# A streaming-encoder layer on one core: one source order for four engines through all 22 matrix blocks, block sums on VectorE, value loads issued by ScalarE

## The chip, the cores and the metric

The kernel runs on one core of one Trainium2 chip. The metric is the device time of one execution in microseconds (us). Before the change the median of 3 runs is 2679.69 us (2674.99 to 2684.86). The engines are called as the profile calls them: PE is TensorE (matmuls; PEld is its weight load), DVE is VectorE, ACT is ScalarE, POOL is GpSimd, SP is SyncE, which here only issues transfers.

## What is computed

One layer on 2048 tokens of width 1024, all float32:

```python
hn = rmsnorm(h, norm_mix_g[l])
proj = hn @ w_in[l]
...
h = h + jnp.concatenate([y_pool, y_dn], axis=-1) @ w_out[l]
m = rmsnorm(mem, mem_norm_g[l])
h = h + memory_cross_attention(rmsnorm(h, norm_xattn_g[l]), m, w_xq[l], w_xk[l], w_xv[l], w_xo[l])
h = h + sqrelu_mlp(rmsnorm(h, norm_mlp_g[l]), w_up[l], w_down[l])
return rmsnorm(h, final_norm_g)
```

`y_pool` is a multi-scale trailing mean, `y_dn` a gated delta rule in chunks. The cross-attention has 256 memory tokens and 4 heads. The MLP is `relu(h @ w_up) ** 2 @ w_down` with an inner width of 4096.

## The kernel before, in words

**First part (to about 873 us).** Projection, convolution, delta rule and the small memory products. The change does not touch it.

**Second part: 22 blocks.** What is left is 22 products of 1024 x 1024 x 1024, here called blocks 0 to 21 (`macros`, lines 872 and 873). Blocks 0 and 1 are the output projection (`o`) of token halves 0 and 1, blocks 2 and 3 the attention scores (`s`), blocks 4 and 5 the product with values and output weights (`v`). Then come, for each token half, four pairs of an up block (`u`) and a down block (`d`): blocks 6 to 13 for half 0, blocks 14 to 21 for half 1.

**Seven steps a block.** Each block is computed by Strassen's scheme in Winograd's form: seven products of 512 x 512 x 512 instead of eight, in the order 1, 2, 6, 7, 5, 4, 3 (`ORDER`). I call the steps of a block index 0 to 6, as the code does. Each float32 operand is split into a high and a low part that PE takes at full rate, and each product is three matmuls: a step is 4 column tiles `t` = 0 to 3 of 12 matmuls, 48 in all. For a step the other engines must do this:

- `loads(n)` (line 883): SP fetches the operand tiles `x` and `t`, two steps ahead. The pool of `t` has 3 buffers.
- `prep(n)` (line 919): ACT casts the two operands to their high parts `sh` and `th` (4 casts of 128 x 1024), DVE subtracts for the low parts `sl` (line 939) and `tl` (line 941). They go to one of two buffer sets (`win`), so a step's operands can be written only when PE has finished the step before the previous one. For the second token half of `s` and `v` the low part `tl` is not computed again: the first half stored it (`lo_s`, `lo_v`), and POOL issues its load (line 933).
- `chains(n)` (line 985): the matmuls into two groups of four PSUM tiles, A and B, and after each `t` an `evac_...` function that adds the result to where it belongs, mostly on DVE (lines 1027, 1044, 1047, 1065).

**Sums.** Steps of index 2 to 5 need sums of quarters of both operands. `adds(k, part)` (line 946) makes those of the left operand, in four parts of two 128 x 1024 operations: on DVE up to block 6 (`NA` is 6) and for `d` blocks, on POOL for the later `u` blocks. `sums(key, ...)` (line 136) makes those of the right operand in 8 units: POOL issues two loads into a tile `cb`, four 128 x 256 operations follow, on DVE up to block 6 and on POOL later, and POOL issues the store to `sums_...`. The keys are `s`, `v`, `n0`, `n1` (normed activations) and `w0` to `w3` (slices of `w_down`). The dictionary `plan` (lines 1149 to 1159) says at which block and index each unit stands.

**Transposes.** In blocks 1 to 6 PE also transposes the previous block's result (`turned`, line 1119); ACT and DVE copy the transposes out (`nr...`), into the same PSUM pools that B uses.

**Who sets the order.** Up to block 6 the order of PE, ACT, DVE and POOL is the order of the source (`step_fixed`, line 1185): within `t` = 0 and 1 of step n the parts of `prep(n + 1)`, then the copies of the transposes, the evacuation of the previous `t`, and so on. From block 7 on (`step_free`, line 1243) only PE keeps the source's order; a scheduler orders the other engines when the kernel is built. In both cases the order is fixed before the run, and each engine takes its instructions one after the other.

```python
    with tc.manual_schedule(engines={E_.PE}):
        with tc.manual_schedule(engines={E_.Activation, E_.DVE, E_.Pool}):
            for n in range(1, 7 * (NA + 1)):
                step_fixed(n)
            close_fixed()
        for n in range(7 * (NA + 1), len(steps)):
            step_free(n)
```

The last `d` block of each half (blocks 13 and 21) also norms the rows and stores them (lines 1048 to 1054): a square on ACT, a power on POOL (line 103), two multiplications on DVE (line 1053) a row tile.

Of the kernel before, what the change touches and what calls it, by code (L numbers as in the profile page):

```python
# [8 lines left out]
F32 = mybir.dt.float32  # L9
# [23 lines left out]
def hymba_layer(ctx: ExitStack, tc: tile.TileContext, x, mem, norm_mix_g, w_in, w_pool, pool_scale, conv_w,  # L33
# [885 lines left out]
    def prep(n):  # L919
# [10 lines left out]
        for i in range(2):  # L930
            T.append([wtile(w_, a, f"{a}_{nm}_{i}", F32R) for a in ("th", "tl")])
            if known:
                nc.gpsimd.dma_start(T[i][1].bitcast(F32), lo_d[kind][LO[j], i])
# [12 lines left out]
    def adds(k, part):  # L946
# [3 lines left out]
        eng = nc.vector if kind == "d" or k <= NA else nc.gpsimd  # L950
# [87 lines left out]
    def evac_add(n, j, t, ps):  # L1038
# [9 lines left out]
        if kind == "d" and g == DFF // D - 1 and j in (4, 3):  # L1048
            jk = jp.tile([P, D], BF16, tag="jk", name=f"fj{sb}_{r + t}")
            rs = rms_scale(jk, h_, f"f{sb}_{r + t}")  # L1050
            for i, gf in enumerate(mac[kind, sb, g]["gf"]):
                hv = h_[:, i * TB:(i + 1) * TB]
                nc.vector.scalar_tensor_tensor(hv, hv, rs, gf, ALU.mult, ALU.mult)
            nc.sync.dma_start(out[sb * D + (r + t) * P:sb * D + (r + t + 1) * P, :], h_)
# [95 lines left out]
    dense = (4, 4, 4, 5, 5, 5, 6, 6)  # L1150
    late = (3, 3, 4, 4, 5, 5, 6, 6)
    full = (2, 2, 3, 3, 4, 4, 5, 5)
    for k, where in (("s", [(0, i) for i in (1, 2, 2, 3, 3, 4, 4, 5)]),
                     ("v", [(b, i) for b in (1, 3) for i in (3, 4, 5, 6)]),
                     ("w0", [(2, i) for i in (1, 3, 4, 5)] + [(6, i) for i in (3, 4, 5, 6)]),
                     ("n0", [(5, i) for i in dense]), ("w1", [(7, i) for i in full]),
                     ("n1", [(8, i) for i in late]), ("w2", [(9, i) for i in full]), ("w3", [(11, i) for i in full])):
        for at in where:
            plan.setdefault(at, []).append(k)
# [7 lines left out]
    def sum_units(i, idx, t=None):  # L1167
# [4 lines left out]
        for k in todo:  # L1172
            if k not in gens:
                gens[k] = sums(k, side_tile, nc.vector if i <= NA else nc.gpsimd, {"s": 3, "n0": 2}.get(k, 1),
                               4 if k in ("v", "w0") else 0)
            next(gens[k])
# [8 lines left out]
    def step_fixed(n):  # L1185
        k, idx = divmod(n, 7)
        mc = macros[k]
        loads(n + 2)
        if idx == 5:
            open_rows(k + 1)  # L1190
        pr = prep(n + 1)
# [4 lines left out]
        for t, ev in enumerate(chains(n)):  # L1196
            if t < 2:
                next(pr, None)
# [9 lines left out]
            if t == 1:  # L1208
# [21 lines left out]
            if idx == 6 and k < NA and t > 1:  # L1230
                adds(k + 1, t - 2)
# [10 lines left out]

    def step_free(n):
        k, idx = divmod(n, 7)
        if n + 2 < len(steps):
            loads(n + 2)
        if n + 1 < len(steps):
            for _ in prep(n + 1):
                pass
        if idx == 0:  # L1250
            if k > NA + 1:
                open_rows(k)
            adds(k, 0)
            adds(k, 1)
        elif idx == 1:
            adds(k, 2)
            adds(k, 3)
        sum_units(k, idx)
        for ev in chains(n):
            after(after(after([ev])))  # L1260
# [54 lines left out]
```

## Time and profile before

| what | value |
|---|---|
| median of 3 runs | 2679.69 us |
| the profiled execution's own time | 2678.6 us |
| its span in the trace | 2676.9 us |
| PE busy | 2558.5 us (96%) |
| DVE busy | 1949.6 us (73%) |
| ACT busy | 1383.3 us (52%) |
| POOL busy | 812.7 us (30%) |
| mean granted clock of PE | 0.98 |

How to read it: PE is busy nearly all the time, so what can be lost or won at its present work is the rest. The profiled execution took 1.7 us more than its span, and 1.1 us less than the median. Busy shares are means over both parts; what a stage waits for is read block by block.

### The profile page before, as it was taken

The page shows a single profiled execution, that of the slowest core. Times are in us where ns is not written, and L with a number is a line of the kernel's source. Part 1 is how long each engine was busy: PE and PEld are TensorE (multiplying, and loading weights), DVE is VectorE, ACT ScalarE, POOL GpSimd, SP SyncE. Part 2 cuts the span into 40 slices and gives each one's busy share as a digit, 9 for nine tenths or more (in the row PEclk, how much of TensorE's full clock was granted, in tenths as well). Part 3 has the DMA queues.
Part 4 walks back from the last instruction along what each step waited for, and adds up shares of the span by engine and source line. Part 5 has one row for each costly group of instructions (what it writes and reads, how often), then busy time and mean ns, then how long its engine had stood idle before and what let it go on. Part 6 is the DMA issues. An engine that isn't in the chain of part 4 may idle for free.

```text
span 2676.9 us, 35124 instructions
## 1 busy us (share of the span) xinstructions
PE 2558.5 (96%) x12822; PEld 2153.5 (80%) x12822; DVE 1949.6 (73%) x2537; ACT 1383.3 (52%) x2286; POOL 812.7 (30%) x863
## 2 busy tenths in 40 slices
PE   7999999999999899998989899999998999999998
PEld 6887789789778788887868788887887888888887
DVE  6865775675685888878657777878688685868666
ACT  7435534635634455875536546363554636455453
POOL 4432455541421311110021477884202101020100
PEclk9999999999999999999989999999999999999999
DMA  4335246234225999988998658673335434233322
GB/s 145 89 105 187 79 146 214 75 107 150 83 84 184 338 342 364 328 319 323 326 351 281 217 182 274 205 249 129 126 128 193 167 108 160 95 127 123 99 99 103
DMA packets 250743, 495.58 MB, mean 185 GB/s; under 512 B 35445, under 2 KB 105674, under 8 KB 250570
## 3 DMA queue, kind: packets, MB, share of 16 engines
q1 hardware_dynamic: 188538, 382.17, 41.9%
q0 software_dynamic: 26048, 90.19, 9.7%
q10 hardware_dynamic: 35984, 20.98, 2.8%
q8 instruction: 100, 1.64, 0.3%
q14 instruction: 73, 0.60, 0.1%
HBM read 371.64 MB, written 121.63 MB: 184 GB/s over the span
## 4 chain that ended last, share of the span: by engine, by line
PE 59%; DVE 8%; DMA 6%; ACT 4%; issue 4%; POOL 2%; POOLq 0%; DVEq 0%; SPq 0%; ACTq 0%
PE A L1009 28%; PE B L1009 21%; DMA t<-vwo_d 1%; DVE tl L941 1%; PE pcm L98 1%; PE pcm L99 1%; PE pcm L97 1%; DVE sl L939 1%; DMA sums_w<-cb_w 1%; DVE cac L385 1%; PE px L498 1%; DMA sums_n<-cb_n 1%; ACT sh L936 1%; DMA cb_n<-n_d 1%; DVE xb L466 1%
## 5 line engine op out<-in xcount | busy, mean ns | idle before, releaser
L1009 PE MATMUL A<-th,sh 128*128 128x512 f32 x1392 | 547.7, 393 | 11.7 <-DVE vr L1044 11.4
L1009 PE MATMUL A<-tl,sh 128*128 128x512 f32 x1392 | 544.0, 391 | 1.4 <-DVE tl L941 0.8
L1009 PE MATMUL A<-th,sl 128*128 128x512 f32 x1392 | 543.6, 391 | 0.0
L1009 PE MATMUL B<-tl,sh 128*128 128x512 f32 x1056 | 416.3, 394 | 21.5 <-DMA tl<-lo_v 10.5
L1009 PE MATMUL B<-th,sh 128*128 128x512 f32 x1056 | 415.7, 394 | 12.6 <-ACT nrs L1137 6.6
L1009 PE MATMUL B<-th,sl 128*128 128x512 f32 x1056 | 415.3, 393 | 0.0
L941 DVE TENSOR_TENSOR tl<-t,th 128x1024 fp32r<-128x1024 f32 x278 | 391.1, 1407 | 12.1 <-ACT th L937 12.1
L937 ACT CAST th<-t 128x1024 fp32r<-128x1024 f32 x306 | 320.6, 1048 | 49.2 <-DMA t<-sums_w 19.1
L1009 PEld LDWEIGHTS A<-th,sh 128*128 128x128 f32 x1392 | 262.6, 189 | 66.1 <-issue 12.1
L1009 PEld LDWEIGHTS A<-tl,sh 128*128 128x128 f32 x1392 | 262.8, 189 | 55.9 <-DVE tl L941 1.6
L939 DVE TENSOR_TENSOR sl<-x,sh 128x1024 fp32r<-128x1024 f32 x166 | 218.5, 1316 | 121.4 <-ACT sh L936 121.4
L1009 PEld LDWEIGHTS A<-th,sl 128*128 128x128 f32 x1392 | 262.4, 188 | 54.8
L936 ACT CAST sh<-x 128x1024 fp32r<-128x1024 f32 x166 | 173.9, 1048 | 214.3 <-PE B L1009 116.0
L1009 PEld LDWEIGHTS B<-tl,sh 128*128 128x128 f32 x1056 | 200.9, 190 | 66.0 <-DMA tl<-lo_v 10.9
L1009 PEld LDWEIGHTS B<-th,sh 128*128 128x128 f32 x1056 | 201.1, 190 | 56.0 <-ACT nrs L1137 6.8
L1009 PEld LDWEIGHTS B<-th,sl 128*128 128x128 f32 x1056 | 201.0, 190 | 42.0
L936 ACT CAST sh<-c 128x1024 fp32r<-128x1024 f32 x96 | 100.8, 1050 | 226.6 <-PE A L1009 121.2
L97 PE MATMUL pcm<-hhi_x,wh_in 128*128 128x512 f32 x512 | 208.1, 406 | 0.2 <-ACT wh_in L90 0.2
L99 PE MATMUL pcm<-hhi_x,wl_in 128*128 128x512 f32 x512 | 205.0, 402 | 2.3 <-DVE wl_in L91 2.2
L98 PE MATMUL pcm<-hlo_x,wh_in 128*128 128x512 f32 x512 | 204.1, 399 | 0.0
L939 DVE TENSOR_TENSOR sl<-c,sh 128x1024 fp32r<-128x1024 f32 x96 | 126.1, 1313 | 68.1 <-ACT sh L936 68.0
L385 DVE SCALAR_TENSOR_TENSOR cac<-raw,vec,cac 128x512 f32<-128x512 f32 x144 | 129.3, 898 | 2.3
(361 smaller groups left out, 4651.9 us busy)
## 6 DMA issues: line engine op xcount, KB each, us to landing
ws_in<-in_w_in_dram SPq DMA_DIRECT2D x72, 512.0 KB, 3.8
x<-in_w_up_dram SPq DMA_DIRECT2D x64, 512.0 KB, 4.4
t<-sums_n SPq DMA_DIRECT2D x64, 512.0 KB, 4.7
t<-sums_w SPq DMA_DIRECT2D x64, 512.0 KB, 3.2
t<-n_d SPq DMA_DIRECT2D x48, 512.0 KB, 4.5
t<-in_w_down_dram SPq DMA_DIRECT2D x48, 512.0 KB, 4.7
cb_w<-in_w_down_dram POOLq DMA_DIRECT2D x64, 256.0 KB, 5.8
sums_w<-cb_w POOLq DMA_DIRECT2D x32, 512.0 KB, 4.2
```

The costliest lines, as they stand in the source:

```text
L97: nc.tensor.matmul(ps, lhsT=lh, rhs=rh, start=first, stop=False)
L98: nc.tensor.matmul(ps, lhsT=lh, rhs=rl, start=False, stop=False)
L99: nc.tensor.matmul(ps, lhsT=ll, rhs=rh, start=False, stop=last)
L385: nc.vector.scalar_tensor_tensor(a5, raw[:, j:j + 512], g_cv[:, j, ch:ch + 1], a5, ALU.mult, ALU.add)
L466: nc.vector.tensor_tensor(xb[:, 0:i, i:32], xb[:, 0:i, i:32], tv, ALU.subtract)
L498: nc.tensor.matmul(px[:, h * P:(h + 1) * P], lhsT=vT[:, h, :], rhs=cur[:, h, :], start=True, stop=True)
L936: nc.scalar.copy(S[i][0], raw[i])
L937: nc.scalar.copy(T[i][0], m["T"][j][i])
L939: nc.vector.tensor_tensor(S[i][1], raw[i], S[i][0].bitcast(F32), ALU.subtract)
L941: nc.vector.tensor_tensor(T[i][1], m["T"][j][i], T[i][0].bitcast(F32), ALU.subtract)
L1009: nc.tensor.matmul(ps, lhsT=l_[:, a0:a0 + P], rhs=r_[:, b0:b0 + TB], start=start and c == 0 and i_ == 0, stop=last and c == 3 and i_ == 2, ...
```

## The change

One body, `step_fixed`, now serves all 22 blocks, and `step_free` is gone. All `adds` go to DVE. Those of `v` and `d` blocks parts 0 and 1 move from the last index of the previous block to index 0 of their own; those of `u` blocks stand in the last index of the block before. At index 1 the copies of the transposes come ahead of the casts. The loads of `lo_v` are issued by ACT. The plan of the sums changes for `v` (second half of its units), `w1`, `w2`, `w3` and `n1`; POOL still computes those from block 7 on. The final norm is cut into two later pieces.

```diff
             if known:
-                nc.gpsimd.dma_start(T[i][1].bitcast(F32), lo_d[kind][LO[j], i])
+                (nc.scalar if kind == "v" else nc.gpsimd).dma_start(T[i][1].bitcast(F32), lo_d[kind][LO[j], i])
...
-        eng = nc.vector if kind == "d" or k <= NA else nc.gpsimd
+        eng = nc.vector
...
-            jk = jp.tile([P, D], BF16, tag="jk", name=f"fj{sb}_{r + t}")
-            rs = rms_scale(jk, h_, f"f{sb}_{r + t}")
...
+            def rest():
+                jk = jp.tile([P, D], BF16, tag="jk", name=f"fj{sb}_{r + t}")
+                rs = rms_scale(jk, h_, f"f{sb}_{r + t}")
+
+                def scaled():
+                    for i, gf in enumerate(mac[kind, sb, g]["gf"]):
...
-                     ("v", [(b, i) for b in (1, 3) for i in (3, 4, 5, 6)]),
...
+    for k, where in (("s", at(0, 1, 2, 2, 3, 3, 4, 4, 5)), ("v", at(1, 3, 4, 5, 6) + at(3, 0, 2, 3, 3)),
+                     ("w0", at(2, 1, 3, 4, 5) + at(6, 3, 4, 5, 6)), ("n0", at(5, 4, 4, 4, 5, 5, 5, 6, 6)),
+                     ("w1", at(7, *range(6)) + at(8, 3, 4)), ("w2", at(8, 5) + at(9, *range(6)) + at(10, 3)),
+                     ("w3", at(10, 4, 5) + at(11, *range(6))), ("n1", at(12, 3, 4, 5) + at(13, *range(5)))):
...
         for t, ev in enumerate(chains(n)):
+            if idx == 1 and t == 0:
+                after(outs)
+                outs[:] = []
...
+            if mc[0] in "dv" and idx == 0 and t > 1:
+                adds(k, t - 2)
...
-            if idx == 6 and k < NA and t > 1:
+            if idx == 6 and more and macros[k + 1][0] not in "dv" and t > 1:
                 adds(k + 1, t - 2)
...
-    with tc.manual_schedule(engines={E_.PE}):
-        with tc.manual_schedule(engines={E_.Activation, E_.DVE, E_.Pool}):
-            for n in range(1, 7 * (NA + 1)):
-                step_fixed(n)
-            close_fixed()
-        for n in range(7 * (NA + 1), len(steps)):
-            step_free(n)
+    with tc.manual_schedule(engines={E_.PE, E_.Activation, E_.DVE, E_.Pool}):
+        for n in range(1, len(steps)):
+            step_fixed(n)
+        close_fixed()
```

**Place 1: POOL in block 5, index 4 to 6, before.** `cb_n` and `sums_n` are units of `n0`, `tl<-lo_v` are the stored low parts that index 6 of the block needs.

```order
L146 DMA cb_n_4_13434<-n_d_90 128x2x256 x2
L171 DMA sums_n_97<-cb_n_2_13392 128x4x256
L933 DMA tl_0_13467<-lo_v 128x1024
L933 DMA tl_1_13470<-lo_v 128x1024
L146 DMA cb_n_5_13496<-n_d_90 128x2x256 x2
L171 DMA sums_n_97<-cb_n_3_13413 128x4x256
```

In the changed kernel the same two loads stand on ACT, right ahead of the casts of the same step (`sh`, `th`):

```order
L933 DMA tl_0_13465<-lo_v 128x1024
L933 DMA tl_1_13468<-lo_v 128x1024
L936 CAST sh_0_13470<-x_36_0_12796 128x1024
L937 CAST th_0_13464<-t_0_13334 128x1024
L936 CAST sh_1_13488<-x_36_1_12798 128x1024
```

The two loads no longer stand behind the store of a unit of `n0`, which waits for DVE.

**Place 2: POOL at the end of block 6, before.** `sums_w_99<-cb_w_7` is the store of the last unit of `w0`, which block 7 needs; `sums_w_100` belongs to `w1`, which block 9 needs.

```order
L171 DMA sums_w_100<-cb_w_0_14560 128x4x256
L146 DMA cb_w_1_14563<-in_w_down_dram 128x2x256 x2
L167 TENSOR_TENSOR cb_w_1_14563<-cb_w_1_14563 128x256
...
L171 DMA sums_w_100<-cb_w_1_14563 128x4x256
L171 DMA sums_w_99<-cb_w_7_14286 128x4x256
L146 DMA cb_w_2_14571<-in_w_down_dram 128x2x256 x2
```

And in the changed kernel:

```order
L171 DMA sums_w_99<-cb_w_6_14199 128x4x256
L171 DMA sums_w_99<-cb_w_7_14284 128x4x256
L146 DMA cb_w_0_14456<-in_w_down_dram 128x2x256 x2
L146 DMA cb_w_1_14459<-in_w_down_dram 128x2x256 x2
L167 TENSOR_TENSOR cb_w_0_14456<-cb_w_0_14456 128x256
```

The store of the last unit of `w0` now stands ahead of all work for `w1`.

**Place 3: DVE at the end of block 13, in the changed kernel.** `x_98`, `x_99` and `n` are quarter sums of block 14, a `u` block, which POOL made before; `L1056` is the final norm (line 1053 before), `L1044` the evacuation of block 13.

```order
L1056 SCALAR_TENSOR_TENSOR vr_7_11933<-vr_7_11933,rs_f_7_18445,gf_1_17866 128x512
L953 TENSOR_TENSOR x_98_0_18290<-x_98_0_18286,x_98_0_18290 128x1024
L953 TENSOR_TENSOR x_98_1_18292<-x_98_1_18288,x_98_1_18292 128x1024
L1044 SCALAR_TENSOR_TENSOR vr_2_11928<-B_2_18211,rv_0_12972,vr_2_11928 128x512
L1056 SCALAR_TENSOR_TENSOR vr_0_11926<-vr_0_11926,rs_f_0_18469,gf_0_17865 128x512
L1056 SCALAR_TENSOR_TENSOR vr_0_11926<-vr_0_11926,rs_f_0_18469,gf_1_17866 128x512
L957 TENSOR_TENSOR n_0_18499<-x_99_0_18385,x_98_0_18290 128x1024
L957 TENSOR_TENSOR n_1_18500<-x_99_1_18387,x_98_1_18292 128x1024
```

Here the sums of the next block stand between the pieces of the norm on one engine; before, they stood on POOL, between its powers.

## Rows read from the trace of the kernel before

**Rows 1.** Stretches by block: us, PE, PEld, DVE, ACT, POOL busy, PEclk, DMA, GB/s.

```profile
962.51:1045.81 83.30, 83.30 (x401) 69.69 (x400) 71.02 (x91) 43.61 (x59) 12.08 (x14) 1.00 0.91 331
...
1130.22:1217.72 87.50, 84.85 (x402) 69.46 (x401) 64.19 (x113) 65.40 (x136) 13.95 (x22) 1.00 0.91 335
1217.72:1309.15 91.43, 84.87 (x402) 70.68 (x401) 70.61 (x94) 43.40 (x64) 2.39 (x4) 0.96 0.92 325
1309.15:1407.90 98.75, 86.59 (x401) 71.62 (x400) 60.16 (x86) 41.91 (x53) 21.94 (x33) 0.93 0.93 333
1407.90:1495.61 87.71, 85.18 (x401) 70.86 (x400) 64.40 (x82) 57.16 (x73) 19.00 (x21) 0.98 0.81 286
...
1495.61:1581.57 85.96, 79.06 (x338) 64.40 (x337) 69.51 (x68) 29.75 (x31) 57.73 (x56) 0.96 0.55 182
...
1657.73:1733.89 76.16, 76.16 (x338) 63.06 (x337) 66.05 (x65) 30.67 (x32) 60.40 (x58) 1.00 0.63 207
...
1810.04:1894.78 84.74, 79.16 (x338) 64.98 (x337) 71.53 (x64) 29.56 (x31) 30.93 (x23) 0.96 0.37 120
...
2047.10:2133.83 86.73, 79.85 (x338) 64.70 (x337) 60.19 (x53) 51.32 (x67) 20.55 (x10) 0.94 0.60 206
```

**Rows 2.** The same view, blocks 19 and 21, down blocks beside which POOL does little.

```profile
2438.45:2514.61 76.16, 76.16 (x338) 63.08 (x336) 62.16 (x65) 30.08 (x32) 5.67 (x2) 1.00 0.29 97
...
2590.81:2667.10 76.29, 76.28 (x337) 62.86 (x335) 61.55 (x70) 31.69 (x43) 3.81 (x6) 1.00 0.27 95
```

**Rows 3.** Waits of PE from 1040 us on: us in total, times, longest.

```profile
PE A L1009 <- DVE vr L1044: 11.4, 2, 5.8
PE B L1009 <- DMA tl<-lo_v: 10.5, 1, 10.5
PE B L1009 <- DVE tl L941: 6.8, 2, 4.2
PE B L1009 <- ACT nrs L1137: 6.6, 1, 6.6
```

**Rows 4.** Chain that ended last, end of block 3: start, us, what.

```profile
1195.39 18.34 DMA t<-vwo_d
```

**Rows 5.** Instructions of POOL in block 5: start, us, what, idle before.

```profile
1361.96 0.53 POOL L933 DMA_DIRECT2D tl<-lo_v  x1 [0.83 <-PE A L1009]
...
1383.07 1.08 POOL L933 DMA_DIRECT2D tl<-lo_v  x2
...
1403.16 1.42 POOL L146 DMA_DIRECT2D cb_n<-n_d  x2 [8.58 <-DMA sums_n<-cb_n]
```

**Rows 6.** Instructions of DVE in block 5.

```profile
1397.39 0.43 DVE L167 TENSOR_TENSOR cb_n<-cb_n 128x256 f32<-128x256 f32 x1 [6.67 <-DMA cb_n<-n_d]
```

**Rows 7.** Instructions of DVE around the start of block 7.

```profile
1499.22 0.41 DVE L170 TENSOR_TENSOR cb_w<-cb_w 128x256 f32<-128x256 f32 x1
```

**Rows 8.** Instructions of POOL around the start of block 7.

```profile
1508.00 0.74 POOL L170 TENSOR_TENSOR cb_w<-cb_w 128x256 f32<-128x256 f32 x1
1509.03 1.53 POOL L171 DMA_DIRECT2D sums_w<-cb_w  x2 [0.30 <-POOL cb_w L170]
```

**Rows 9.** Instructions of DVE in block 11.

```profile
1832.35 3.61 DVE L960 TENSOR_TENSOR c<-n,c 128x1024 f32<-128x1024 f32 x1
```

**Rows 10.** Instructions of POOL in block 11.

```profile
1832.43 2.43 POOL L957 TENSOR_TENSOR n<-x,x 128x1024 f32<-128x1024 f32 x1
```

**Rows 11.** Instructions of DVE between blocks 13 and 14.

```profile
2042.31 3.55 DVE L1053 SCALAR_TENSOR_TENSOR vr<-vr,rs_f,gf 128x512 f32<-128x512 f32 x2
```

**Rows 12.** Groups of instructions of DVE in block 19: busy us, mean ns, idle before.

```profile
L941 DVE TENSOR_TENSOR tl<-t,th 128x1024 fp32r<-128x1024 f32 x14 | 18.9, 1351 | 0.0
...
L1044 DVE SCALAR_TENSOR_TENSOR dr<-A,rv,dr 128x512 f32<-128x512 f32 x16 | 11.8, 748 | 4.4 <-PE A L1009 4.4
...
L953 DVE TENSOR_TENSOR c<-c,c 128x1024 f32<-128x1024 f32 x2 | 2.4, 1224 | 1.3 <-ACT c L1032 1.3
```

**Rows 13.** Stores of yT_d: ns min, median, max of the issue, first and last start.

```profile
L601 ACTq DMA_DIRECT2D yT_d<-yst x16: 366/367/399, 199.9 to 887.5; - x16
```

More of the change, by code (lines that the diff above doesn't have):

```diff
@@ L1048, in evac_add @@
         if kind == "d" and g == DFF // D - 1 and j in (4, 3):
-            jk = jp.tile([P, D], BF16, tag="jk", name=f"fj{sb}_{r + t}")
-            rs = rms_scale(jk, h_, f"f{sb}_{r + t}")
[L1051 to L1054, printed above, removed]
+            def rest():
[3 more added lines that the diff above has]
+                    for i, gf in enumerate(mac[kind, sb, g]["gf"]):
+                        hv = h_[:, i * TB:(i + 1) * TB]
+                        nc.vector.scalar_tensor_tensor(hv, hv, rs, gf, ALU.mult, ALU.mult)
+                    nc.sync.dma_start(out[sb * D + (r + t) * P:sb * D + (r + t + 1) * P, :], h_)
+                return scaled
+            return rest
     def evac_sc(n, j, t, ps):
@@ L1149, in hymba_layer, with at @@
     plan = {}
[L1150 to L1153, printed above, removed]
-                     ("v", [(b, i) for b in (1, 3) for i in (3, 4, 5, 6)]),
[L1155 to L1159, printed above, removed]
+    def at(b, *idx):
+        return [(b, i) for i in idx]
+    for k, where in (("s", at(0, 1, 2, 2, 3, 3, 4, 4, 5)), ("v", at(1, 3, 4, 5, 6) + at(3, 0, 2, 3, 3)),
+                     ("w0", at(2, 1, 3, 4, 5) + at(6, 3, 4, 5, 6)), ("n0", at(5, 4, 4, 4, 5, 5, 5, 6, 6)),
+                     ("w1", at(7, *range(6)) + at(8, 3, 4)), ("w2", at(8, 5) + at(9, *range(6)) + at(10, 3)),
+                     ("w3", at(10, 4, 5) + at(11, *range(6))), ("n1", at(12, 3, 4, 5) + at(13, *range(5)))):
+        for w_ in where:
+            plan.setdefault(w_, []).append(k)
     gens, now = {}, [0]
@@ L1174, in sum_units @@
                 gens[k] = sums(k, side_tile, nc.vector if i <= NA else nc.gpsimd, {"s": 3, "n0": 2}.get(k, 1),
-                               4 if k in ("v", "w0") else 0)
+                               {"v": 4, "w0": 4, "w1": 6, "w2": 7}.get(k, 0))
             next(gens[k])
@@ L1187, in step_fixed @@
         mc = macros[k]
-        loads(n + 2)
+        more = k + 1 < len(macros)
+        if n + 2 < len(steps):
+            loads(n + 2)
         if idx == 5:
             open_rows(k + 1)
-        pr = prep(n + 1)
+        pr = prep(n + 1) if n + 1 < len(steps) else iter(())
         side = 0 < k <= NA
@@ L1241, in close_fixed @@
         after(outs)
[L1243 to L1260, printed above, removed]
     loads(0)
```

## The prediction

> **What bounds the kernel now.** Read the second part block by block. The first view is the table of stretches, one row a block [rows 1]. Block 1 takes 83.30 us with PE busy throughout: that is what a block with transposes costs when nothing makes PE wait. Block 9 takes 76.16 us, the same for a block without them; ten more of blocks 7 to 21 have that length. So PE bounds the blocks at 83.3 and 76.16 us, and a gain can come only from what single blocks take above that: block 3 4.2 us, block 4 8.1, block 5 15.45, block 6 4.4, block 7 9.8, block 11 8.6, block 14 10.6 [rows 1]; together 61.2 us. Block 2 is 1.1 over, block 0 is filled by a start that the change leaves alone. Not all of an excess is idle time: block 5 idles 98.75 - 86.59 = 12.2 us, and the other 3.3 us are matmuls that run longer, at a granted clock of 0.93; in blocks 7, 11 and 14 the clock is 0.96, 0.96 and 0.94. PE stood before these stretches, and a wait that goes takes the slow stretch behind it along.
>
> The second view, the waits of PE, names who ended the idle time: the loads of `lo_v` once for 10.5 us, the evacuations `vr` on DVE twice for 11.4, `tl` on DVE twice for 6.8, the copies `nrs` on ACT once for 6.6 [rows 3]. Then I followed each of these back through the instructions of the engine named. After the last matmul 9.8 us remain (2667.1 to 2676.9) [rows 2].
>
> **Blocks 3 and 4 (12.3 us over).** In block 3 the operand load `t<-vwo_d`, issued at 1195.39, takes 18.34 us [rows 4]; DVE then does late what stands behind it: the sums of block 4, a unit of `v`, the evacuations, and last the operands and copies that PE waits for. The change takes both loads off this place: units of `v` leave index 4 to 6 of block 3 for index 0 to 3, and the two sums (four operations of 1.22 us [rows 12], 4.9 us) go to index 0 of block 4. Three units that stood there move 0.5 MB in and 0.5 MB out each, 3 MB or 9 us at 335 GB/s [rows 1]; two of them fall before the load's landing, so it should land some 6 us sooner, and DVE has 6 us less to do behind it. At index 1 the copies of the transposes now come ahead of the casts. What remains late is DVE in index 0 of block 4, where the sums now stand. I take 10 of 12.3 us; bounds 3 and 12.
>
> **Blocks 5 and 6 (19.9 us over).** In index 3 the loads of `lo_v` are issued when PE frees the buffer, the second at 1361.96; those for index 6 come only at 1383.07, behind a store of `n0` [rows 5], about 10 us after the buffer was free. ACT will issue them on time. The price is issue time on ACT, 0.37 us a load [rows 13], two a step, plus ACT's wait for the buffer, which the casts behind it need anyway; ACT is busy 41.9 of 98.75 us [rows 1], so this is hidden. So the 10.5 us go. But DVE is late next: it stands before a unit of `n0` until 1397.39 [rows 6], and the operands of block 6 come behind that, about 1402. PE will want them at about 1395. The last load of `n0` is issued at 1403.16 after 8.58 us for a store [rows 5], and the first sums of block 6 use a buffer of the same pool. DMA runs at 333 GB/s here, more than in block 4 [rows 1]. So half of it comes back as a wait for the units: I take 9 us; bounds 0 (the units set the pace as before) and 17.
>
> **Block 7 (9.8 us).** DVE finishes the last unit of `w0` at 1499.6 [rows 7], but POOL issues the store only at 1509 to 1510.6, behind two units of `w1` [rows 8]; block 7 needs it. In the new order it stands ahead of them: 10 us earlier. I take 9; bounds 5 and 9.8.
>
> **Block 11 (8.6 us).** DVE's sum of 128 x 1024 takes 3.61 us [rows 9] instead of 1.22 [rows 12], while POOL does one of 2.43 us from 1832.43 on [rows 10]. Those POOL operations (8 in each `u` block from block 8 on) disappear, and are 8 operations of 1.22 us on DVE. A `u` block leaves DVE room: 3 of its 7 evacuations are DVE's, against 7 in a `d` block. I take 8.5; bounds 4 and 8.6.
>
> **Block 14 (10.6 us).** Two multiplications of the final norm take 3.55 us [rows 11] where two of such form take 1.5 [rows 12], again beside POOL's sums. The change removes that, but puts the sums between the pieces of the norm on DVE: index 6 of block 13 gets four evacuations (3.0 us), four subtractions (2 x 1.35 + 2 x 1.22 = 5.1), eight multiplications (6.0) and four sums (4.9), 19 us in a step of 10.88 (a seventh of 76.16). It ends 8 us late. Operands are normally done some 6 us before PE needs them, so about 2 us remain. I take 8.5; bounds 3 and 10.6.
>
> **After the last matmul.** The last evacuations stood behind older norms; take 1 us, bounds 0 and 2.
>
> **What is added.** In index 6 of each down block the sums of the next up block make 3.0 + 5.1 + 4.9 = 13 us of DVE's work in 10.88 us, and index 0 of each down block the same: 2 us late, inside the 6 us. Over a whole block: block 19 keeps DVE busy 62.2 us [rows 2], with four sums more 67.1. In blocks 7, 9, 11 and 13 POOL makes 5 or 6 units beside it. Block 9 of before, with 8 units (60.4 us of POOL), has DVE at 66.05 us, 3.9 more than block 19 [rows 1, 2]; six units are 2.9 us, so 70 of 76.16. I take 1 us for small new waits; bounds 0 and 10.
>
> The Trainium skill (SBUF — State Buffer, "SBUF: two separate sides") speaks against this: it calls the port that VectorE and GpSimd share an exclusive lock, and says that the one that starts second blocks fully. The 3.61 us in block 11 agree. If DVE were always the one that blocks, six units of four operations of 0.74 us alone [rows 8] would cost DVE 17.8 us a block, and 67.1 + 17.8 = 84.9 would pass 76.16. By block 9 POOL mostly loses: its units took 60 us there. I go by the row; the other is the second rival.
>
> **The sum.** 10 + 9 + 9 + 8.5 + 8.5 + 1 - 1 = 45 us. The profiled execution took 2678.6, so 2633.6; the median stands 1.1 above it: 2634.7 us.
>
> **The rivals.**
> - *The transfers bound blocks 3 to 6.* For: 325 to 335 GB/s in three blocks on end [rows 1], loads that take 18 us [rows 4]. Against: block 1 ran at PE's pace with 331 GB/s. Then 10 + 9 come to nothing, and the time is 2653.7.
> - *The lock goes against DVE in the down blocks with units.* Blocks 7, 9 and 11 go 8.7 us over, block 13 with 5 units 5.8: 32 us, 2667. Against: block 9 [rows 1].
> - *No wait is left but block 0's.* All 61.2 + 1.1 us and the tail's 1 go: 2616.
> - *Slower: DVE breaks step.* The place is index 6 of the seven down blocks before an up block (7 to 19), where 13 us stand in 10.88. It decides if DVE comes there already 4 us late, for then operands pass the 6 us of slack. If each costs what the late blocks 7, 11 and 14 cost now, 9.7 us on the mean, that is 68 us: 2703. Against: blocks 9 and 19 show DVE idle 10 us and more [rows 1, 2].
>
> That the order would not change is no rival: the three places above show that it does.
>
> **How the numbers follow.** Forecast 0.65, transfers 0.10, lock 0.10, no wait left 0.10, slower 0.05. A measurement of this kernel can tell about 0.5% (13 us) from no change. The forecast, the first and the third rival are faster by more; the second (0.5%) counts half as faster, half as no change; the last is slower. So 0.90 faster, 0.05 same, 0.05 slower. The terms' lower bounds taken for two of them at once (blocks 5 and 6 none, block 14 3 us) give 2649, and new waits of 10 us 2658; the upper ones 2617. The range 2616 to 2660 takes in these, the forecast, the first and third rival.
>
> **What would show it right or wrong.** Right: blocks 7, 8, 10, 11 and 12 at 76.2 us, no 128 x 1024 operations on POOL after block 6, loads of `lo_v` issued every 11 to 14 us through block 5, block 4 under 86 us, blocks 5 and 6 together 10 to 12 us above 166.6 with DVE waiting for `cb_n`, block 14 about 78. Wrong: a down block over 78 us with `tl` or `vr` as releaser (lock, or broken step), blocks 5 and 6 unchanged (transfers), or a DVE busy time in blocks 7, 9, 11 above 72 us.

## The result, and the profile after

The changed kernel takes 2645.69 us (median of 4 runs, 2643.81 to 2648.08), the kernel before, run beside it on the same chip, 2678.26 us. The ratio is 0.9876 with a 95% interval of 0.9854 to 0.9898: 1.2% faster, well beyond the 0.5% that can be told from no change. The prediction was 2634.7 us with a range of 2616 to 2660: right in its sign and inside its range, 11.0 us too low. Profiled execution against profiled execution (2647.18 to 2633.6) it is 13.6 us: the prediction put the median 1.1 us above the profiled one, and it lies 1.5 below. The profiled execution took 2647.18 us, its span is 2645.4 us, and the mean granted clock 0.988.

The stretches of blocks 3, 4, 5, 6, 7, 11 and 14 after the change, in the columns of [rows 1] (us, busy time of PE, PEld, DVE, ACT and POOL, granted clock, DMA share, GB/s):

```profile
1128.79:1218.70 89.91, 86.19 (x401) 70.33 (x400) 67.20 (x122) 66.59 (x141) 14.71 (x23) 0.98 0.97 352
1218.70:1303.92 85.22, 83.86 (x402) 69.64 (x400) 65.29 (x83) 41.30 (x59) 0.00 (x0) 1.00 0.89 317
1303.92:1393.38 89.46, 86.42 (x401) 71.79 (x400) 53.05 (x77) 40.37 (x50) 13.87 (x19) 0.96 0.91 324
1393.38:1493.61 100.23, 88.55 (x401) 72.47 (x400) 72.74 (x95) 59.77 (x76) 11.76 (x17) 0.93 0.82 287
1493.61:1569.77 76.16, 76.16 (x337) 63.06 (x336) 66.88 (x67) 29.32 (x31) 46.09 (x43) 1.00 0.57 187
...
1798.25:1874.41 76.16, 76.16 (x337) 63.06 (x336) 67.87 (x68) 29.33 (x31) 38.18 (x33) 1.00 0.51 166
...
2026.73:2103.63 76.90, 76.50 (x337) 63.00 (x336) 54.82 (x57) 51.88 (x65) 6.01 (x3) 1.00 0.70 237
```

Read against [rows 1]: blocks 7 and 11 are at the 76.16 us that a block without transposes costs, block 14 0.74 us above; each was 8.6 to 10.6 us over. Block 5 is 9.3 us shorter, but block 6 is 12.5 us longer, and block 3 2.5 us. Taken from first matmul to first matmul, blocks 1 to 6 are 533.1 us before and 533.2 after; blocks 7 to 21 are 1171.5 before and 1143.3 after. So the whole gain, but for 3.4 us in block 0, the start and the tail, lies behind block 6.

Waits of PE from 1040 us on, after the change (us in total, times, longest), against [rows 3]:

```profile
PE ptv L1136 <- DVE vr L1047: 4.5, 1, 4.5
PE A L1009 <- DVE tl L941: 3.7, 1, 3.7
PE A L1009 <- DMA tl<-lo_s: 3.6, 3, 2.7
PE B L1009 <- ACT nrv L1146: 3.5, 1, 3.5
PE B L1009 <- DVE nrv L1150: 3.0, 1, 3.0
```

The wait of 10.5 us for `lo_v` is gone. Three of the waits in its place (`tl`, `vr`, and `nrv` on ACT, 11.7 us) stand in index 0 of block 6, which takes 27.67 us, where PE alone needs 12.57. The rest of block 6's excess is matmuls that run longer after PE stood: PE is busy 88.55 us in it where 83.30 do, at a granted clock of 0.93. Followed back on DVE (start, us, what, idle before and who ended it):

```profile
1392.15 0.42 DVE L167 TENSOR_TENSOR cb_n<-cb_n 128x256 f32<-128x256 f32 x1 [1.17 <-DMA cb_n<-n_d]
...
1405.44 1.22 DVE L957 TENSOR_TENSOR n<-x,x 128x1024 f32<-128x1024 f32 x1
1412.03 1.22 DVE L957 TENSOR_TENSOR n<-x,x 128x1024 f32<-128x1024 f32 x1 [5.37 <-DMA sums_n<-cb_n]
...
1414.89 0.68 DVE L1047 TENSOR_TENSOR vr<-B,vr 128x512 f32<-128x512 f32 x1
```

DVE stands twice behind the units of `n0`: for their fetches, and, 5.37 us long, in the second sum of block 6 (L957), whose result goes to a buffer that a unit still holds until its store has landed. The evacuation `vr`, for which the transposes wait, is queued behind it. POOL shows the pace of the units:

```profile
1380.05 1.42 POOL L146 DMA_DIRECT2D cb_n<-n_d  x2 [5.58 <-DMA sums_n<-cb_n]
...
1391.20 1.42 POOL L146 DMA_DIRECT2D cb_n<-n_d  x2 [4.58 <-DMA sums_n<-cb_n]
...
1401.78 1.42 POOL L146 DMA_DIRECT2D cb_n<-n_d  x2 [8.38 <-DMA sums_n<-cb_n]
```

Each fetch waits for an earlier store to land and free its buffer. The DMA engines are full while this goes on; in stretches of 10 us (columns as above):

```profile
1390.00:1400.00 10.00, 6.31 (x23) 4.52 (x21) 8.14 (x12) 6.45 (x11) 2.19 (x3) 0.88 1.03 402
...
1410.00:1420.00 10.00, 3.12 (x14) 2.18 (x12) 7.86 (x10) 6.21 (x12) 0.75 (x1) 0.73 0.47 177
```

From 1410 us on they are half idle, and PE still stands. That leaves two readings of blocks 5 and 6: the order of work on DVE and the units' chain (called A, C and G below, as they were sharpened), or the transfers (B).

### The profile page after: what moved, and what is told of

The parts are those of the page before. It is cut to its first block, busy times and chain, and to the rows that moved or that the text cites. A ratio compares the mean times of both kernels' runs of the same rounds, so it can differ in the third digit from the quotient of the medians.

```text
span 2645.4 us, 34978 instructions
## 1 busy us (share of the span) xinstructions
PE 2549.4 (96%) x12822; PEld 2148.9 (81%) x12822; DVE 1938.8 (73%) x2593; ACT 1386.1 (52%) x2286; POOL 672.9 (25%) x793
## 4 chain that ended last, share of the span: by engine, by line
PE 66%; DVE 6%; DMA 4%; issue 2%; ACT 2%; POOL 1%; ACTq 0%; DVEq 0%; SPq 0%; POOLq 0%
PE A L1009 33%; PE B L1009 24%; PE pcm L98 1%; PE pcm L99 1%; PE pcm L97 1%; DMA sums_n<-cb_n 1%; DVE cac L385 1%; PE px L498 1%; DMA tl<-lo_s 1%; DVE tl L941 1%; DVE xb L466 1%; DVE sl L939 0%; PE pto L1136 0%; DMA t<-sums_v 0%; PE ptv L1136 0%
## 5 line engine op out<-in xcount | busy, mean ns | idle before, releaser
L941 DVE TENSOR_TENSOR tl<-t,th 128x1024 fp32r<-128x1024 f32 x278 | 355.6, 1280 | 4.0 <-ACT th L937 4.0
L939 DVE TENSOR_TENSOR sl<-x,sh 128x1024 fp32r<-128x1024 f32 x166 | 206.1, 1242 | 75.1 <-ACT sh L936 75.0
L103 POOL TENSOR_TENSOR rs_f<-rs_f,mhalf 128x1 f32<-128x1 f32 x16 | 17.0, 1063 | 628.8 <-ACT rs_f L102 628.8
L939 DVE TENSOR_TENSOR sl<-c,sh 128x1024 fp32r<-128x1024 f32 x96 | 118.8, 1237 | 39.3 <-ACT sh L936 39.3
```

The costliest lines, as they stand in the source:

```text
L103: nc.gpsimd.tensor_tensor(dst, dst, mhalf[:, :dst.shape[-1]], ALU.pow)
L939: nc.vector.tensor_tensor(S[i][1], raw[i], S[i][0].bitcast(F32), ALU.subtract)
L941: nc.vector.tensor_tensor(T[i][1], m["T"][j][i], T[i][0].bitcast(F32), ALU.subtract)
```

## The experiments

Block lengths (first matmul to first matmul, in us, profiled execution) of all kernels; each ratio is against runs of the kernel before on the same chip.

| kernel | median us | ratio (95%) | block 3 | 4 | 5 | 6 | 7 to 21 |
|---|---|---|---|---|---|---|---|
| before | 2678.26 | 1 | 87.45 | 91.45 | 98.81 | 87.69 | 1171.5 |
| changed | 2645.69 | 0.9876 (0.9854 to 0.9898) | 89.92 | 85.21 | 89.47 | 100.23 | 1143.3 |
| e1 first blocks only | 2676.28 | 0.9985 (0.9970 to 1.0000) | 90.69 | 85.23 | 87.09 | 101.36 | 1172.8 |
| e2 MLP only | 2649.18 | 0.9882 (0.9862 to 0.9902) | 87.51 | 92.51 | 96.85 | 90.57 | 1143.3 |
| e3 `n0` units on POOL | 2651.22 | 0.9890 (0.9869 to 0.9912) | 91.05 | 85.22 | 87.27 | 102.06 | 1143.3 |
| e4 no `lo_v` transfers | 2637.42 | 0.9837 (0.9820 to 0.9855) | 90.93 | 86.08 | 83.31 | 94.61 | 1143.3 |
| e5 adds of block 6 later | 2644.87 | 0.9871 (0.9856 to 0.9885) | 90.33 | 85.25 | 89.61 | 96.08 | 1143.3 |
| e6 e4 and e5 | 2637.90 | 0.9843 (0.9827 to 0.9860) | 90.51 | 85.25 | 83.31 | 94.29 | 1143.3 |
| e7 sums of `u` on POOL | 2676.91 | 0.9989 (0.9974 to 1.0003) | 89.75 | 85.21 | 89.49 | 96.65 | 1174.7 |
| e8 old places of MLP units | 2692.52 | 1.0045 (1.0029 to 1.0060) | 90.77 | 85.21 | 86.99 | 100.94 | 1189.4 |
| e9 no `n0` units | 2630.40 | 0.9815 (0.9802 to 0.9829) | 90.37 | 85.21 | 89.25 | 83.31 | 1143.3 |
| e10 four buffers, e5 | 2642.59 | 0.9860 (0.9845 to 0.9875) | 90.15 | 85.21 | 87.82 | 95.08 | 1143.3 |
| e11 e4, e10, `lo_s` on ACT | 2631.20 | 0.9812 (0.9799 to 0.9825) | 87.49 | 89.46 | 83.31 | 89.99 | 1143.3 |
| e12 `lo_v` on POOL | 2650.13 | 0.9885 (0.9868 to 0.9901) | 90.10 | 85.23 | 101.46 | 88.67 | 1143.3 |

How well a block length repeats can be read from e7 and e8, which give the engines the same work in the same order as the changed kernel up to block 6: blocks 5 and 6 together take 186.1 and 187.9 us there, and 189.7 in the changed kernel. With one profiled execution of each kernel, a difference below 4 us in these two blocks is therefore not read as an effect.

### Which half of the change gains (e1, e2)

e1 puts the edits to the first blocks into the kernel before:

```diff
-                nc.gpsimd.dma_start(T[i][1].bitcast(F32), lo_d[kind][LO[j], i])
+                (nc.scalar if kind == "v" else nc.gpsimd).dma_start(T[i][1].bitcast(F32), lo_d[kind][LO[j], i])
...
+                     ("v", [(1, i) for i in (3, 4, 5, 6)] + [(3, i) for i in (0, 2, 3, 3)]),
...
+            if mc[0] == "v" and idx == 0 and t > 1:
+                adds(k, t - 2)
...
```

> The kernel before with only the change's edits to the first seven blocks (value's low parts fetched by ScalarE, the unit plan of v, the adds of a value block in its own first step, the last transposes sent out a chain earlier); the MLP stays with the scheduler and its adds on GpSimd. Theory A (order): these edits only trade one wait for another, VectorE standing behind the n0 units. Theory B (transfers): blocks 1 to 6 are as long as their bytes. Both: blocks 1 to 6 together 530 to 536 us as in both kernels (533.1 and 533.2), blocks 7, 11 and 14 at 85 to 87, and 2675 to 2682 in all. If instead the first terms of the prediction hold without the new MLP, blocks 1 to 6 come to 514 and the whole to about 2660.

e2 takes the same edits out of the changed kernel:

```diff
-            if idx == 1 and t == 0:
+            if idx == 1 and t == 0 and k > NA:
...
-            if mc[0] in "dv" and idx == 0 and t > 1:
+            if mc[0] == "d" and idx == 0 and t > 1:
...
```

> The changed kernel with blocks 0 to 6 put back as they were before (low parts of value fetched by GpSimd, the old places of the v units, adds of value blocks in the step ahead); blocks 7 to 21 as changed. Both theories: blocks 7 to 21 as in the changed kernel, 76.2 each with 76.9 in block 14, about 28 us less than before; blocks 1 to 6 at 533 +- 3; 2647 to 2652 in all, no slower than the changed kernel by over 4 us. If the first six blocks carry part of the changed kernel's gain, it is 2655 or more.

Both came out as expected, but for blocks 7 and 11 of e1, 89.65 and 83.04 us where 85 to 87 were expected. In e1 blocks 1 to 6 take 532.6 us and the whole does not differ from before by what can be told; block 6 has the long index 0 of the changed kernel (27.73 us). In e2 the MLP alone brings 0.9882, and its blocks 7 to 21 are the changed kernel's to 0.1 us. The median of e2 is 3.5 us above the changed kernel's, and the intervals overlap widely. The terms for blocks 3 to 6 are thus not lost to some interplay with the MLP: those edits bring nothing by themselves.

### What gains in the MLP (e7, e8)

```diff
-        eng = nc.vector
+        eng = nc.gpsimd if kind == "u" and k > NA else nc.vector
```

> The changed kernel with the quarter sums of the up blocks after block 6 put back on GpSimd, in the fixed order (8 operations of 128x1024 a block, four of them in index 6 of the down block ahead). Theory D (collision): a VectorE operation beside such a GpSimd one takes about 3 us instead of 1.2, as before the change, and waits of 3 to 9 us come back in two or more of blocks 9 to 21; 2655 to 2680 in all. Theory E (the fixed order alone brought the gain): blocks 8 to 13 and 15 to 21 stay at 76.2, 2644 to 2649 in all.

With this single line undone all of the gain is gone, though not block by block: block 7 keeps its 76.16 us, and blocks 8, 9, 11 and 14 take 84.1, 84.2, 79.9 and 88.5 us (76.16, 76.16, 84.7 and 86.7 before). DVE at the end of block 7, then POOL beside it:

```profile
1560.07 0.74 DVE L1044 SCALAR_TENSOR_TENSOR vr<-B,rv,vr 128x512 f32<-128x512 f32 x1
1560.73 12.25 DVE L939 TENSOR_TENSOR sl<-x,sh 128x1024 fp32r<-128x1024 f32 x1
1572.90 1.21 DVE L941 TENSOR_TENSOR tl<-t,th 128x1024 fp32r<-128x1024 f32 x1
```

```profile
1560.15 4.76 POOL L953 TENSOR_TENSOR x<-x,x 128x1024 f32<-128x1024 f32 x2
1564.85 4.74 POOL L957 TENSOR_TENSOR n<-x,x 128x1024 f32<-128x1024 f32 x2
1569.55 2.33 POOL L960 TENSOR_TENSOR x<-n,x 128x1024 f32<-128x1024 f32 x1
```

One DVE subtraction of 1.21 us takes 12.25: it begins 0.6 us after the first of five POOL operations has begun, and ends 1.1 us after the last has ended. PE then waits 5.3 us for the `tl` behind it. So the collision of [rows 9, 10] is real, and a fixed order doesn't cure it. The Trainium skill (SBUF — State Buffer, "SBUF: two separate sides") has the two engines lock a shared port, with the second to start blocked for the whole of the other's instruction. These rows agree, with one thing more: the wait went over five instructions in a row. In [rows 9, 10] only the length of the wait agrees (1.22 and 2.43 make 3.65 us, measured 3.61); DVE's record begins 0.08 us ahead of POOL's there and DVE is still the one that waits.

```diff
-                     ("w1", at(7, *range(6)) + at(8, 3, 4)), ("w2", at(8, 5) + at(9, *range(6)) + at(10, 3)),
+                     ("w1", at(7, 2, 2, 3, 3, 4, 4, 5, 5)), ("w2", at(9, 2, 2, 3, 3, 4, 4, 5, 5)),
```

(and `w3` and `n1` likewise, in blocks 11 and 8, with the limits on how far ahead the units of `w1` and `w2` are fetched put back as well)

> The changed kernel with the units of w1, w2, w3 and n1 at the places they had before (eight in each of blocks 7, 8, 9 and 11, two to a step), in the fixed order. Theory E (the fixed order and the adds on VectorE brought the gain, not the units' places): blocks 7 to 14 within 1 us of the changed kernel's, 2643 to 2650 in all. Theory F (the thinner spread of the units brought it): block 7 or 11 is 4 to 10 us longer again, 2650 to 2665.

Neither theory had the place or the size: the kernel is no faster than before, by its interval 0.3 to 0.6% slower. Blocks 7, 11 and 14 keep their gain, but block 8 takes 86.7 us and block 10 111.7. DVE at the end of block 9, and the last of POOL's units there:

```profile
1732.51 0.74 DVE L1044 SCALAR_TENSOR_TENSOR vr<-B,rv,vr 128x512 f32<-128x512 f32 x1
1769.65 1.35 DVE L957 TENSOR_TENSOR n<-x,x 128x1024 f32<-128x1024 f32 x1 [36.40 <-DMA sums_w<-cb_w]
```

```profile
1752.56 1.41 POOL L146 DMA_DIRECT2D cb_w<-in_w_down_dram  x2 [2.89 <-DMA sums_w<-cb_w]
...
1761.11 1.42 POOL L146 DMA_DIRECT2D cb_w<-in_w_down_dram  x2 [2.91 <-DMA sums_w<-cb_w]
```

POOL needs 8.5 us for a unit (1752.56 to 1761.11) even while DVE stands; two to a step of 10.88 us are too many. The second sum, now at a fixed place on DVE, takes its buffer from the pool of the units and so waits until nearly all eight are through, 36.40 us, with the evacuations behind it. Block 8 has the same wait, of 11.28 us. So the sums on DVE and the thin spread of units belong together: the one takes the collisions away, and the other keeps that gain from being lost. It is the same wait, in the same line L957, that stands in block 6.

### Where the gain of blocks 5 and 6 went (e12, e3, e5, e4, e6, e9, e10, e11)

```diff
-                (nc.scalar if kind == "v" else nc.gpsimd).dma_start(T[i][1].bitcast(F32), lo_d[kind][LO[j], i])
+                nc.gpsimd.dma_start(T[i][1].bitcast(F32), lo_d[kind][LO[j], i])
```

> The changed kernel with value's low parts fetched by GpSimd again, and nothing else undone. Theory G (the end of index 0 of block 6 is set by the chain of the n0 units, whatever PE waits for before it): the loads stand behind n0 stores again, PE waits 8 to 12 us for them in index 6 of block 5, and index 0 of block 6 falls from 27.7 to 14 to 20 us; blocks 5 and 6 within 5 us of 189.7, 2641 to 2651 in all. If the late issue was a cost of its own, as the prediction had it, blocks 5 and 6 grow by 8 to 11 us to 198 or more, 2653 to 2657.

The wait for the low parts came back (8.8 us, 10.5 before), index 0 of block 6 fell from 27.67 to 16.52 us, and blocks 5 and 6 take 190.1 us against 189.7 (the other 2.5 us between the two spans lie outside them). Waits of PE from 1040 us on:

```profile
PE B L1009 <- DMA tl<-lo_v: 8.8, 1, 8.8
PE B L1009 <- DVE nrv L1150: 7.1, 2, 3.7
```

So the issue by ACT does what it says, and gains next to nothing in these blocks, where a cost of its own would have shown as 8 to 11 us. The medians lie 4.4 us apart, with intervals that overlap (0.9868 to 0.9901 and 0.9854 to 0.9898). Whatever PE waits for ahead of it, the end of index 0 of block 6 is set elsewhere.

```diff
-                gens[k] = sums(k, side_tile, nc.vector if i <= NA else nc.gpsimd, {"s": 3, "n0": 2}.get(k, 1),
+                gens[k] = sums(k, side_tile, nc.vector if i <= NA and k != "n0" else nc.gpsimd, {"s": 3, "n0": 2}.get(k, 1),
```

> The changed kernel with the subtractions of the eight n0 units on GpSimd in place of VectorE: same bytes, same buffers, but VectorE's queue no longer stands behind their fetches. Theory A (order): VectorE evacuates in time, blocks 5 and 6 together fall from 189.7 to 176 to 182 us, 2632 to 2639 in all. Theory B (transfers): blocks 5 and 6 within 4 us of 189.7, 2641 to 2650 in all.

By its block lengths this went to the transfers: blocks 5 and 6 take 189.3 us (the median, 2651.22 us, lies 1.2 above the range of that theory too). But DVE shows why it could not tell the two apart; its queue still stands behind the units, in the sums:

```profile
1401.31 1.23 DVE L957 TENSOR_TENSOR n<-x,x 128x1024 f32<-128x1024 f32 x1 [7.26 <-issue]
1413.10 1.23 DVE L957 TENSOR_TENSOR n<-x,x 128x1024 f32<-128x1024 f32 x1 [10.57 <-DMA sums_n<-cb_n]
```

(For the 7.26 us the trace names no releaser.) So the sums were moved behind the evacuations:

```diff
-            if mc[0] in "dv" and idx == 0 and t > 1:
+            if (mc[0] in "dv" or k == NA) and idx == 0 and t > 1:
...
-            if idx == 6 and more and macros[k + 1][0] not in "dv" and t > 1:
+            if idx == 6 and more and macros[k + 1][0] not in "dv" and k + 1 != NA and t > 1:
```

> The changed kernel with the first two adds of block 6 moved from index 6 of block 5 to index 0 of block 6, as the value and down blocks have them. Theory C (a buffer wait at the head of VectorE's queue): the second add waits for a buffer that an n0 store holds (5.4 us in the changed kernel, 10.6 with the units on GpSimd, 6.2 without the low parts), and the evacuations, operands and norms behind it are late by as much; moved behind them, index 0 of block 6 falls from 27.7 to 15 to 20 us, blocks 5 and 6 from 189.7 to 178 to 185, 2635 to 2641 in all. Theory B (transfers): the units are as late as before, and what index 0 gains index 1 or 2 loses; blocks 5 and 6 within 3 us of 189.7, 2642 to 2649.

A miss for theory C: the wait in L957 is gone, index 0 still takes 23.34 us, and the median is 0.8 us below the changed kernel's. Blocks 5 and 6 are 4.0 us shorter in the profiled execution, a little more than theory B allowed and hardly more than e7's 3.5 without any edit there. The releaser of PE's longest wait is now `nrv`, 7.4 us.

```diff
-        known = kind in "sv" and sb > 0
+        known = kind == "s" and sb > 0
...
-                if kind in "sv":
+                if kind == "s":
```

> The changed kernel with the low parts of value's second operand worked out again in block 5 by VectorE (14 subtractions of 128x1024 more) instead of being stored in block 4 and fetched in block 5: 14 stores and 14 loads of 0.52 MB fewer, 14.7 MB in all, which at the 0.36 MB per us of the full stretches is 40 us of transfers. Theory A (order): the n0 units and the buffers behind them are as they were; blocks 4 to 6 within 5 us of 274.9, 2640 to 2651 in all. Theory B (transfers): blocks 4 to 6 shrink by 15 us or more, 2631 or less in all.

With the adds where the change has them. Between the two theories: blocks 4 to 6 take 264.0 us against 274.9, 10.9 less, at 2637.42 us. Block 5 falls to 83.31 us, the length of a block with transposes and no wait of PE. In the changed kernel ACT waits there for an operand (start, us, what, idle before):

```profile
1311.23 1.05 ACT L937 CAST th<-t 128x1024 fp32r<-128x1024 f32 x1 [5.93 <-DMA t<-vwo_d]
```

Without `lo_v` this wait does not occur. e4 takes the bytes off the DMA engines and also 14 stores off SP's queue, ahead of the operand loads; which of the two counts more was not tried apart. The loads themselves land faster: from 1217 to 1310 us `t<-vwo_d` takes 5.0 us in the median from issue to landing, 6.2 in the changed kernel, and `x<-pT_d` 8.6 against 10.2. Here, 14 subtractions more on DVE cost less than 14.7 MB of transfers in a stretch where the DMA engines are full. Block 6 keeps 11.3 us over 83.3. e6 is this diff and the one ahead of it, the later sums, together:

> Both edits: low parts of value worked out again instead of stored and fetched, and the adds of block 6 in its own index 0. Theory C together with B: with the transfers gone block 5 is at its floor (83.5 in the run without low parts) and the wait at the head of VectorE's queue (6.2 us there) goes too; block 6 from 94.8 to 84 to 88, 2627 to 2631 in all. Theory B alone: block 6 stays at 93 to 96, 2635 to 2639.

A miss for the later sums, and what the transfers alone would give: block 6 stays at 94.29. The wait moved from the second sum to a unit's fetch, on DVE again:

```profile
1400.11 0.42 DVE L167 TENSOR_TENSOR cb_n<-cb_n 128x256 f32<-128x256 f32 x1 [6.30 <-DMA cb_n<-n_d]
```

and POOL issued that fetch late because a store had to land first:

```profile
1392.97 1.43 POOL L146 DMA_DIRECT2D cb_n<-n_d  x2 [9.12 <-DMA sums_n<-cb_n]
```

So the units as a whole were left out, with the reading steps fed from another source; this kernel leaves out a part of the product:

```diff
-            if j in (1, 2, 3):
-                kh, nh = {1: (0, 0), 2: (1, 0), 3: (1, 1)}[j]
+            if j in (1, 2, 3) or key == "n0":
+                kh, nh = {1: (0, 0), 2: (1, 0), 3: (1, 1)}.get(j, (0, 1))
...
-                     ("w0", at(2, 1, 3, 4, 5) + at(6, 3, 4, 5, 6)), ("n0", at(5, 4, 4, 4, 5, 5, 5, 6, 6)),
+                     ("w0", at(2, 1, 3, 4, 5) + at(6, 3, 4, 5, 6)), 
```

> The changed kernel with the eight n0 units of block 5 left out (8.4 MB of fetches and stores, their subtractions and their buffers); the steps that read their sums read a quarter of the normalized rows of the same size instead, so that part of the product is not computed. Theory G (the chain of the units, fetch, subtraction, store, on four buffers, sets the end of index 0 of block 6): block 6 falls from 100.2 to 83 to 85 us; block 5, whose excess stands in index 0 and 1, ahead of the units, stays at 87 to 90; 2627 to 2632 in all. Theory B (the transfers in general): block 6 keeps a third or more of its 17 us, 89 us or longer, since the units are 8.4 MB of some 35 in block 5.

This is what theory G gave: block 6 is at 83.31 us with the `lo_v` transfers still there, and block 5 as long as in the changed kernel. The units' 8.4 MB are gone with them. Stretches of blocks 5 and 6:

```profile
1309.36:1398.61 89.25, 85.18 (x402) 70.85 (x400) 55.44 (x68) 42.73 (x54) 0.00 (x0) 0.98 0.89 304
1398.61:1481.91 83.30, 83.30 (x401) 69.68 (x400) 57.96 (x72) 57.39 (x73) 8.07 (x11) 1.00 0.78 267
```

So block 5's excess (6.2 us over 83.3) belongs to the `lo_v` loads and stores, and block 6's (16.9) to the units. How much of the latter is waiting for buffers, and how much the pace of their transfers, e10 and e11 try:

```diff
-        if now[0] < NA and not (nm[:5] == "cb_n0" and nm[-1] in "135"):
+        if now[0] < NA and not (nm[:5] == "cb_n0" and nm[-1] in "1357"):
```

(with the later sums of e5)

> The changed kernel with the adds of block 6 in its own index 0, and with the buffer of the last n0 unit taken from the pool of the second sums, so that units alternate between the two pools and unit 7 waits for the store of unit 3 rather than of unit 4. Theory G: the wait for the last fetch (6 us on VectorE without the low parts) goes, index 0 of block 6 from 23.3 to 14 to 18 us, 2636 to 2641 in all. Theory B: the last fetch is issued earlier and lands as late; index 0 stays at 21 us or more, 2642 to 2647.

Index 0 takes 22.51 us against 23.34 in e5: as theory B had it, though the median lies 2.3 us below e5's, at the edge of what the runs resolve. The cause is not a fetch that lands late: POOL issues the last one at 1391.24, 0.3 us ahead of block 6 (in e5 at 1399.65, 3.8 us into it), and DVE waits for no unit after it. What ends last now is an operand of index 1, for which ACT stands (7.40 us in e5, where DVE still waited for a unit beside it):

```profile
1406.56 1.05 ACT L937 CAST th<-t 128x1024 fp32r<-128x1024 f32 x1 [9.15 <-DMA t<-n_d]
```

SP had issued this load at 1393.65, 12.9 us earlier, in a stretch of 400 GB/s. So with the last unit's buffer free sooner the units no longer hold index 0 up, and an operand load among full transfers holds it up almost as long. e11 takes the `lo_v` traffic away as well; it has the edits of e4, e5 and e10, and

```diff
-                (nc.scalar if kind == "v" else nc.gpsimd).dma_start(T[i][1].bitcast(F32), lo_d[kind][LO[j], i])
+                nc.scalar.dma_start(T[i][1].bitcast(F32), lo_d[kind][LO[j], i])
```

> Four edits on the changed kernel: the two of the run with alternating buffers, the low parts of value worked out again instead of stored and fetched, and the low parts of the score blocks fetched by ScalarE. Expected by theory G with B: block 3 from 90 to 86 to 88 us (its low parts no longer stand behind a store on GpSimd's queue), block 4 at 85.4, block 5 at 83.5, block 6 at 84 to 90; 2622 to 2631 in all, faster than both kernels. If the transfers alone set block 6, it stays at 94 and the whole at 2633 to 2638.

Index 0 of block 6 takes 16.62 us (20.95 in e6), block 6 89.99. On POOL the fetches are issued at 1380.68 and 1385.95, where e6 has the last at 1392.97:

```profile
1380.68 1.43 POOL L146 DMA_DIRECT2D cb_n<-n_d  x2 [2.73 <-DMA sums_n<-cb_n]
...
1385.95 1.42 POOL L146 DMA_DIRECT2D cb_n<-n_d  x2 [3.07 <-DMA sums_n<-cb_n]
```

At 2631.20 us (5 runs, 2626.91 to 2633.55), 0.2 above the upper end of what was expected, this is the fastest full kernel of the study, 14.5 us below the changed one, and their intervals against before do not touch. ACT still waits 7.59 us for the load of that operand. One of its four edits gains nothing: with `lo_s` issued by ACT block 3 loses its wait (87.49), but block 4 takes 89.46 against 85.2; blocks 3 and 4 together are 176.9 us, against 175.4 in e10. Leaving that edit out was not tried.

## Why the prediction was right, and where it was not

| term | predicted us | measured us |
|---|---|---|
| blocks 3 and 4 | 10 (3 to 12) | 3.8 |
| blocks 5 and 6 | 9 (0 to 17) | -3.2 |
| block 7 | 9 (5 to 9.8) | 9.8 |
| block 11 | 8.5 (4 to 8.6) | 8.6 |
| block 14 | 8.5 (3 to 10.6) | 9.8 |
| tail | 1 (0 to 2) | 1.3 |
| new waits | -1 (-10 to 0) | none in blocks 7 to 21; -0.7 in blocks 1 and 2 |
| block 0 and the start | not in the sum | 2.1 |

The time is inside the range because the MLP's terms came out near their upper bounds, and because the range was wide enough for blocks 5 and 6 to give nothing. Of the 19 us that the prediction took for blocks 3 to 6, 0.6 came. Its upper terms are summed wrongly: they make 60 us and so 2619.7, not 2617; the range does not change by it.

**Blocks 7, 11, 14.** Right, in place and size. The store of `w0` that [rows 8] show at 1509.03, 13.4 us into block 7, is issued at 1493.79, 0.2 us into it; in e1, which leaves that order alone, block 7 stays long. The cause of blocks 11 and 14, the collision of [rows 9, 10], is shown by e7: the sums back on POOL cost 31.4 us in blocks 7 to 21, 3.7 of them in block 11, 11.6 in block 14, and 8.0 each in blocks 8 and 9, which were at 76.16 before. Block 14 was forecast to keep 2 us; it keeps 0.7.

**The failed step: blocks 5 and 6.** The prediction had the 10.5 us for `lo_v` go and "half of it" come back as a wait for the units, bounded at nothing below. All of it came back: the two blocks take 189.7 us, 23.1 above 166.6, where the prediction's own sign was 10 to 12 (the 3.2 us over the kernel before are within what e7 and e8 vary by). The step that failed is the one that took the late issue on POOL for a cost of its own. e12 shows that it is worth 0.4 us in these blocks, to within that spread: the units of `n0` end when they end, and PE waits for them in block 6 or for something else just ahead. The rows said so: a last fetch issued at 1403.16 behind 8.58 us for a store, and sums of block 6 in the units' pool [rows 5]. The prediction named them and still gave the term half its price.

**Blocks 3 and 4.** The place was right and block 4 gave its 6.2 us, but block 3 took 2.5 back. On POOL after the change:

```profile
1185.19 0.76 POOL L171 DMA_DIRECT2D sums_v<-cb_v  x1 [5.54 <-DVE cb_v L170]
1185.94 1.09 POOL L933 DMA_DIRECT2D tl<-lo_s  x2
```

And the same loads before it:

```profile
1182.99 1.08 POOL L933 DMA_DIRECT2D tl<-lo_s  x2
```

The low parts of the scores are issued right behind a store of `v` for which POOL stood 5.54 us, and PE waits 2.7 us for one of them: they are issued 57.2 us after block 3's first matmul, 52.8 us after it before the change. The units, now at index 0, 2 and 3, put two more stores ahead of these loads. The prediction counted what DVE is spared and not whom the moved units stand before on POOL. e11 shows that taking the loads off that queue only moves the wait on, to block 4.

**The rivals.** The sum of blocks 3 to 6, 0.6 us, is what the first rival, transfers, gave for them. Its cause is half right: e4 shows block 5's excess to come with the `lo_v` traffic, and e9 block 6's with the units, a chain of fetch, subtraction and store on four buffers which full DMA engines make slow. e10 shows that an operand load in the same full stretch stands right behind that chain. The profiled execution came 5.4 us below the 2652.6 us that this rival gives for it: 0.6 us from blocks 3 to 6, 2.4 from the other terms' surplus, 1.0 from new waits that did not come, 2.1 from block 0 and the start, less 0.7 in blocks 1 and 2. The lock against DVE in down blocks and the slower case did not come: DVE is busy 66.9, 66.8 and 67.9 us in blocks 7, 9 and 11, and no down block is over 76.2 us but the last, which has its 76.3 of before. e8 shows a way to the slower side at the place which that rival named, index 6 of the down blocks; but what decides there is a buffer, and not DVE's load.

What stays open: how much of index 0 of block 6 an earlier issue of its operand loads would give with the transfers left as they are, which was not tried, and why block 3's wait only moved to block 4 in e11.

## What to carry to other kernels

Before pricing a wait that an edit removes, find what ends next in the same stretch and remove both on paper: here a load issued 10 us too late cost next to nothing, because a chain of units, and an operand load right behind it, ended no sooner. When work moves to an engine with a fixed order, look for every instruction whose output buffer another engine has to free; it stands at the head of that queue, and all behind it waits (5.4, 10.6 and 36.4 us here). In a stretch where the DMA engines are full, working an intermediate out again can beat storing and fetching it: 14 subtractions for 14.7 MB gave 8.3 us.

## What the runs showed of the hardware

One DVE operation of 1.21 us took 12.25 us beside five POOL operations of 128x1024 that followed each other without a gap (e7); beside units of 128x256 in the changed kernel it can be POOL that loses, with 2.85 us for an operation of 0.76, while two sums on DVE take 2.35 us as they do alone:

```profile
1499.55 0.76 POOL L167 TENSOR_TENSOR cb_w<-cb_w 128x256 f32<-128x256 f32 x1 [0.62 <-DMA cb_w<-in_w_down_dram]
1500.38 2.85 POOL L168 TENSOR_TENSOR cb_w<-cb_w 128x256 f32<-128x256 f32 x1
```

In the kernel before, both lost beside such units (DVE 1.75 us for 1.22, POOL 1.60 for 0.74, from 1827 to 1832 us).

The stretch of 10 us shown above reaches 402 GB/s where the whole of blocks 5 and 6 of the same kernel shows 324 and 287: a mean over a block hides that the DMA engines are full for part of it and half idle for another.
